# Shift and scale vectors of a two-layer trunk's second layer: partition sums as rows, turned into columns by way of DRAM

## The chip, the cores and the metric

The kernel runs on one core of one Trainium2 chip. The metric is the time of one execution on the device in microseconds, lower is better.

## The reference

A trunk of two layers works on x of 256 rows and 2048 columns, in f32. The token mixer of layer 0 is an attention with forget gates over 16 heads of 128, that of layer 1 a sliding-window attention over 32 query heads of 64. Behind each mixer comes a gated FFN of width 5632 with a convolution over three rows. Both sub-layers of a layer are modulated by vectors that come from a conditioning vector c of 2048 values:

```
c_act = silu(c)
for i in range(2):
    mod = c_act @ ada_w[i] + ada_b[i]                 # ada_w[i]: 2048 x 12288
    sh1, sc1, g1, sh2, sc2, g2 = split(mod, 6)
    y = mixer_i(x * (1 + sc1) + sh1)
    x = layer_norm(alpha * x + (1 + g1) * y)
    y = conv_ffn(x * (1 + sc2) + sh2)
    x = layer_norm(alpha * x + (1 + g2) * y)
```

The change concerns `c_act @ ada_w[1]` for the four vectors sh1, sc1, sh2 and sc2 of layer 1.

## The kernel before, in words

**Weights.** All weights are streamed once from DRAM in f32. `stream` (L277) does it by tiles of two blocks of 128 rows and 512 columns (256 rows of the weight): SP loads `w` (L288) into one of the slots that `wtile` hands out, ACT rounds it to `wh` (L290, f32r), DVE forms the residual `wl = w - wh` (L302), and PE multiplies with both (L76), the first factor being split in the same way. Residuals are recorded two tiles ahead. In the down-projection of the FFN (PE rows `xs<-wh,gT` and `xs<-wl,gT`) the output x is worked off in four d blocks of 512 columns. A tile there is eight matmuls by `wh` and four by `wl`; in the up-projection (`wd`) it is the same number of products in other shapes.

**Between the tiles.** Behind each tile `tick` takes a step of the adaLN work at a set rate, and once per tile `run_post` takes a step of every generator that was handed to `defer`. Such generators carry the additions into x (`residual`, L673): multiply the sum in PSUM by the gate (`t`, L686), add it into x (L687), take statistics (L689).

**The end of a sub-layer.** For the last d block `x_mm_end` (L339) takes the last tiles in another order: row block t = 0 (rows 0 to 127, 512 columns wide) over all of them first, then row block t = 1 in two halves of 256 columns. The last additions into x are pinned on DVE in the order: t = 1 of the tiles before, t = 0 with its statistics and moments (L694), first half, second half with the moments of t = 1. POOL takes the root (`rs`, L698), ACT and DVE normalise x (L714, L716), PE transposes it (L564) between a few dummy matmuls (`warm`), and the modulated h (`hHL`) starts the next sub-layer.

**The adaLN vectors.** `ada_vector` (L442) makes one vector of 2048 values at a time, in the order of `ada_list` (L439): (0,2), (0,3), (0,4), (0,5), (1,0), (1,1), (1,3), (1,2), (1,4), (1,5), layer first. For each block of 128 rows of `ada_w` DVE multiplies by the 128 values of silu(c) and adds into `acc` (128 partitions x 2048, L454 and L456), one half of the row per step. Then the 128 partitions must be summed. Gates (v = 2 and 5) are wanted along the row on every partition: four f32 matmuls with a 128 x 128 block of ones give 128 x 512 each (L469). Shifts and scales (v = 0, 1, 3, 4) are wanted as columns, 128 partitions x 16: for each of 16 pieces of 128 columns one f32 matmul with `acc` as the stationary factor and one column of ones as the moving one, all into one PSUM bank, four of them to a step (L477), and at the end one DVE instruction that adds the bias (`cv`, L481). Both are pinned, that is, they keep their place among the pinned instructions of their engine. `merged` (L743) later makes the modulation's G and B from these columns.

**What sets the order.** The kernel is written in the Tile framework. Its scheduler orders the instructions of each engine; pinned ones keep the order in which they were recorded, others may be moved, and the slots of a pool go to those who ask in scheduled order. PSUM has 8 banks of one pool. In the profile, layer 0's FFN lies between 460 and 1211 us; the sums of (1,0), (1,1) and (1,3) fall into it (first blocks at 798.36, 939.48 and 1092.87), those of (1,4) into layer 1's output projection (first block at 1445.56).

Of the kernel before, what the change touches and what calls it, by code (L numbers as in the profile page):

```python
# [10 lines left out]
F32 = mybir.dt.float32  # L11
# [3 lines left out]
ALU = mybir.AluOpType  # L15
AX = mybir.AxisListType

P = 128
D = 2048
S = 256  # L20
NT = S // P
KC = D // P
# [19 lines left out]
def hybrid_trunk(ctx: ExitStack, tc: tile.TileContext, a: dict, out: bass.AP):  # L42
    nc = tc.nc
# [5 lines left out]
    cst = ctx.enter_context(tc.tile_pool(name="cst", bufs=1))  # L49
# [2 lines left out]
    gp = ctx.enter_context(tc.tile_pool(name="gp", bufs=31))  # L52
    tp = ctx.enter_context(tc.tile_pool(name="tp", bufs=4))
    sp = ctx.enter_context(tc.tile_pool(name="sp", bufs=4))
    psp = ctx.enter_context(tc.tile_pool(name="psp", bufs=8, space=bass.MemoryType.PSUM))

    def wtile(name="w"):
        return wp.tile([P, 2, WB], F32, tag="w", name=name)
# [7 lines left out]
    def bank(name="sm"):  # L66
        return psp.tile([P, 512], F32, tag="ps", name=name)
# [7 lines left out]
    def mm(o, lhsT, rhs, start=False, stop=False, **kw):  # L75
        return nc.tensor.matmul(o, lhsT, rhs, start=start, stop=stop, **kw)  # L76

    def pin(ins, on=True):

        if on:  # L80
            tc.keep_in_program_order(ins)
# [17 lines left out]
    ident = cst.tile([P, P], F32, name="ident")  # L99
# [3 lines left out]
    ones = cst.tile([P, P], F32, name="ones")  # L103
# [20 lines left out]
    pt = bank()  # L124
    nc.tensor.transpose(pt[:, :KC], csil, ident[:KC, :KC])
    nc.vector.tensor_copy(cact, pt[:, :KC])
    acol = cst.tile([P, DEPTH, NADA], F32, name="acol")
    pt = bank()
# [125 lines left out]
    def defer(gen):  # L254

        post.append(gen)
# [180 lines left out]
    cols = {}  # L437
    gates = {}
    ada_list = [(0, 2), (0, 3), (0, 4), (0, 5), (1, 0), (1, 1), (1, 3), (1, 2), (1, 4), (1, 5)]  # L439
    ada = {"gen": None, "debt": 0.0, "rate": 0.0, "gate_free": True}  # L440

    def ada_vector(l, v):  # L442
        row = v % 3 == 2
        acc = cst.tile([P, D], F32, tag="acc", name="acc")
        part = lambda c, n: acc[:, c:c + n]
        step_ = D // 2
        for k in range(KC):
            for c in range(0, D, D // 2):
                w = wtile("wa").rearrange("p a f -> p (a f)")
                pin(nc.sync.dma_start(w, a["ada_w"][l, k * P:(k + 1) * P, v * D + c:v * D + c + D // 2]), False)  # L450
                for o in range(0, D // 2, step_):
                    ac, wo = part(c + o, step_), w[:, o:o + step_]
                    if k == 0:
                        pin(nc.vector.tensor_scalar_mul(ac, wo, cact[:, 0:1]), True)  # L454
                    else:
                        pin(nc.vector.scalar_tensor_tensor(ac, wo, cact[:, k:k + 1], ac,  # L456
                                                           op0=ALU.mult, op1=ALU.add), True)
                yield
        for _ in range(2 if l == 0 else 0):
            yield  # L460
        if row:
            while not ada["gate_free"]:
                yield
            ada["gate_free"] = False
            g = cst.tile([P, D], F32, tag="gate", name="gate")
            nc.gpsimd.dma_start(g, a["ada_b"][l, v * D:(v + 1) * D].partition_broadcast(P))
            for j in range(D // 512):
                ps = bank()
                mm(ps, ones, acc[:, j * 512:(j + 1) * 512], start=True, stop=True)  # L469
                yield  # L470
                gj = g[:, j * 512:(j + 1) * 512]
                nc.vector.scalar_tensor_tensor(gj, ps, 1.0, gj, op0=ALU.add, op1=ALU.add)
            gates[l, v] = g
            return
        ps = bank()
        for k in range(KC):
            pin(mm(ps[:, k:k + 1], part(k * P, P), ones[:, 0:1], start=True, stop=True))  # L477
            if k % 4 == 3:
                yield
        cv = cst.tile([P, KC], F32, tag=f"cv{v}", name="cv")  # L480
        pin(nc.vector.scalar_tensor_tensor(cv, ps[:, :KC], 1.0 if v % 3 else 0.0,  # L481
                                           acol[:, l, v * KC:(v + 1) * KC], op0=ALU.add, op1=ALU.add), True)
        cols[l, v] = cv
        if v == 4:
            ada["held"] = True

    def ada_step():
        if ada["gen"] is None:
            if not ada_list or ada.get("held"):
                return  # L490
            ada["gen"] = ada_vector(*ada_list.pop(0))
        if next(ada["gen"], ada) is ada:
            ada["gen"] = None
# [730 lines left out]
    for t in range(NT):  # L1224
        mu, rs, _ = moments[t]
# [34 lines left out]
```

## Time and profile before

| | us |
|---|---|
| median of 3 runs | 2235.91 |
| lowest and highest | 2234.55, 2236.51 |
| the profiled execution | 2237.59 |
| its span in the profile | 2235.8 |

| engine | busy us | share |
|---|---|---|
| PE (matmul) | 2196.5 | 98% |
| DVE | 1860.3 | 83% |
| ACT | 1193.4 | 53% |
| POOL | 20.3 | 1% |

The granted clock of PE was 0.998 on the mean. A row of the groups gives line, engine, operation and operands (out<-in), the count, then busy time in us, the mean of one in ns, and the idle time ahead of it with what ended it. A row of the timeline gives start, length, and what; neighbours of one kind are merged with their count. An f32 matmul appears as two passes.

### The profile page before, as it was taken

What the parts mean: (1) busy time and instruction counts of PE and PEld (TensorE: products, weight loads), DVE (VectorE), ACT (ScalarE), POOL (GpSimd) and SP (SyncE); (2) the same over time, 40 slices, a digit from 0 to 9 for tenths busy, and PEclk for the clock granted to TensorE, in tenths of its full rate; (3) what the DMA queues carried; (4) which work ended last, traced back from release to release, by engine and by line L of the source; (5) the groups of instructions that cost most, each with busy time, mean ns of one, the idle gap of its engine ahead of it and who ended that gap; (6) DMA issues with size and microseconds to landing.
All of it is one profiled execution on the core that took longest, in us unless ns stands there. A gap on an engine that the chain in (4) does not pass through costs nothing.

```text
span 2235.8 us, 33537 instructions
## 1 busy us (share of the span) xinstructions
PE 2196.5 (98%) x12275; PEld 1890.3 (85%) x12275; DVE 1860.3 (83%) x2705; ACT 1193.4 (53%) x1877; POOL 20.3 (1%) x51
## 2 busy tenths in 40 slices
PE   7999999999999999999999999999999999999998
PEld 6999898788888888888887788888888888888886
DVE  7989998999979968989899888879888655676766
ACT  4546554455556433656534588646655533555642
POOL 0001000000000000000000000000000000000000
PEclk9999999999999999999999999999999999999999
DMA  9999999979878989889798766668887556666553
GB/s 358 391 355 345 356 374 343 308 256 321 310 226 284 339 287 339 280 273 324 257 341 301 233 199 245 216 195 289 284 263 251 182 194 191 192 190 190 189 197 114
DMA packets 287430, 602.69 MB, mean 270 GB/s; under 512 B 21846, under 2 KB 55576, under 8 KB 286752
## 3 DMA queue, kind: packets, MB, share of 16 engines
q1 hardware_dynamic: 286208, 595.86, 78.3%
q0 software_dynamic: 1056, 4.69, 0.6%
q8 instruction: 96, 1.57, 0.3%
q14 instruction: 70, 0.57, 0.1%
HBM read 598.37 MB, written 2.10 MB: 269 GB/s over the span
## 4 chain that ended last, share of the span: by engine, by line
PE 82%; DVE 11%; issue 3%; ACT 2%; DMA 2%; POOL 0%; SPq 0%; DVEq 0%; ACTq 0%; POOLq 0%
PE wd L76 41%; PE xs L76 32%; PE ws L76 4%; DVE acc L456 3%; DVE wl L302 3%; DMA wo<-in_ada_w_dram 2%; PE sm L76 1%; ACT wh L290 1%; PE o L76 1%; PE S L76 1%; ACT pr L775 1%; DVE pr L763 0%; DMA w<-in_fox_w_in_dram 0%; ACT pr L767 0%; PE cps L76 0%
## 5 line engine op out<-in xcount | busy, mean ns | idle before, releaser
L290 ACT CAST wh<-w 128x1024 fp32r<-128x1024 f32 x728 | 764.2, 1052 | 754.5 <-PE wd L76 269.9
L302 DVE TENSOR_TENSOR wl<-w,wh 128x1024 fp32r<-128x1024 f32 x728 | 886.8, 1222 | 281.4 <-ACT wh L290 262.1
L76 PE MATMUL wd<-hHL,wh 128*128 128x512 f32 (+1 forms) x2832 | 718.3, 395 | 0.3
L76 PEld LDWEIGHTS wd<-hHL,wh 128*128 128x128 f32 x2832 | 504.5, 188 | 98.8 <-issue 2.6
L76 PEld LDWEIGHTS wd<-hHL,wl 128*128 128x128 f32 x2816 | 373.1, 188 | 31.4 <-DVE wl L302 0.6
L456 DVE SCALAR_TENSOR_TENSOR acc<-wa,cact,acc 128x1024 f32<-128x1024 f32 x300 | 381.3, 1279 | 0.1
L76 PE MATMUL wd<-hHL,wl 128*128 128x256 f32 x2816 | 379.7, 277 | 0.2 <-DVE wl L302 0.2
L76 PE MATMUL xs<-wh,gT 128*128 128x512 f32 (+1 forms) x1444 | 352.0, 384 | 0.0
L76 PEld LDWEIGHTS xs<-wh,gT 128*128 128x128 f32 x1444 | 266.8, 188 | 53.0
L76 PE MATMUL xs<-wl,gT 128*128 128x512 f32 (+1 forms) x722 | 191.4, 384 | 0.0
L76 PE MATMUL xs<-wh,hHL 128*128 128x512 f32 (+1 forms) x720 | 185.2, 395 | 0.9 <-ACT hHL L85 0.5
L76 PEld LDWEIGHTS xs<-wl,gT 128*128 128x128 f32 x722 | 134.4, 188 | 26.8
L76 PEld LDWEIGHTS xs<-wh,hHL 128*128 128x128 f32 x720 | 128.6, 188 | 28.1 <-issue 1.4
L1147 ACT ACTIVATE u<-s,ccol 128x256 f32<-128x256 f32 x176 | 105.3, 600 | 65.7 <-DVE s L1142 50.0
L76 PE MATMUL ws<-hHL,wh 128*128 128x256 f32 x1024 | 132.0, 281 | 4.9 <-ACT wh L290 2.4
L76 PEld LDWEIGHTS ws<-hHL,wh 128*128 128x128 f32 x1024 | 124.3, 189 | 8.8 <-ACT wh L290 4.2
L76 PE MATMUL xs<-wh,oT 128*128 128x512 f32 (+1 forms) x392 | 101.3, 396 | 0.0
L76 PE MATMUL xs<-wl,hHL 128*128 128x512 f32 (+1 forms) x360 | 97.3, 390 | 1.7 <-DVE wl L302 1.7
L1148 DVE SCALAR_TENSOR_TENSOR u<-s,ccol,u 128x255 f32<-128x255 f32 x176 | 84.1, 479 | 6.2 <-ACT u L1147 6.0
L609 DVE SCALAR_TENSOR_TENSOR oacc<-wo,cact,oacc 128x512 f32<-128x512 f32 x111 | 79.4, 746 | 10.2 <-DMA wo<-in_ada_w_dram 5.4
L1150 DVE SCALAR_TENSOR_TENSOR u<-s,ccol,u 128x254 f32<-128x254 f32 x176 | 84.0, 478 | 1.4
L76 PEld LDWEIGHTS xs<-wh,oT 128*128 128x128 f32 x392 | 71.1, 190 | 13.7 <-DVE oT L86 0.3
(223 smaller groups left out, 1645.2 us busy)
## 6 DMA issues: line engine op xcount, KB each, us to landing
w<-in_ffn_w_up_dram SPq DMA_DIRECT2D x352, 512.0 KB, 4.6
wa<-in_ada_w_dram SPq DMA_DIRECT2D x320, 512.0 KB, 5.1
w<-in_ffn_w_down_dram SPq DMA_DIRECT2D x176, 512.0 KB, 4.6
w<-in_fox_w_in_dram SPq DMA_DIRECT2D x96, 512.0 KB, 6.6
wo<-in_ada_w_dram SPq DMA_DIRECT2D x128, 256.0 KB, 6.7
w<-in_swa_w_in_dram SPq DMA_DIRECT2D x40, 512.0 KB, 5.0
w<-in_fox_w_o_dram SPq DMA_DIRECT2D x32, 512.0 KB, 5.5
w<-in_swa_w_o_dram SPq DMA_DIRECT2D x32, 512.0 KB, 5.3
```

The source lines that it names most:

```text
L76: return nc.tensor.matmul(o, lhsT, rhs, start=start, stop=stop, **kw)
L290: pin(nc.scalar.copy(h, w), casts[0] > 0)
L302: pin(nc.vector.tensor_tensor(l, w, f32(h), op=ALU.subtract), go in behind or tied[0] > 0)
L456: pin(nc.vector.scalar_tensor_tensor(ac, wo, cact[:, k:k + 1], ac, op0=ALU.mult, op1=ALU.add), True)
L609: nc.vector.scalar_tensor_tensor(ac, wk, cact[:, kc:kc + 1], ac, op0=ALU.mult, op1=ALU.add)
L775: nc.scalar.mul(pr[:, b:e], pr[:, b:e], ss[:, r:r + 1])
L1147: nc.scalar.activation(u, s, AF.Identity, bias=cw(CW, f), scale=cw(2, f))
L1148: nc.vector.scalar_tensor_tensor(u[:, 1:], s[:, :S - 1], cw(1, f), u[:, 1:], op0=ALU.mult, op1=ALU.add)
L1150: nc.vector.scalar_tensor_tensor(u[:, 2:], s[:, :S - 2], cw(0, f), u[:, 2:], op0=ALU.mult, op1=ALU.add)
```

## The change

For layer 1 the four shift and scale vectors are summed in another form. For each of four pieces of 512 columns of `acc` one f32 matmul with a single column of ones as stationary factor gives a row of 1 x 512 in a PSUM bank of its own. ACT copies each row to one partition of a tile (`line`, two rows to a tile), and POOL stores two tiles of 1024 values to a scratch row in DRAM. A deferred generator, `turned`, waits a step, has POOL load the 2048 values back as 16 rows of 128 (`lines`), waits three steps more, lets PE transpose them to 128 x 16, and DVE adds the bias. It replaces 64 column matmuls by 16 row matmuls, 16 ACT copies, 8 stores, 4 loads and 4 transposes. Neither the new matmuls nor the new `cv` are pinned. Layer 0's vectors and the gates stay as they are. Line numbers behind the new code are 29 higher in the kernel after, those ahead of it 1 higher.

```
+    dp = ctx.enter_context(tc.tile_pool(name="dp", bufs=2, space=bass.MemoryType.DRAM))
...
+        if l > 0:
+            line, r = dp.tile([D // 1024, 1024], F32, name="line"), None
+            for j in range(D // 512):
+                ps = bank()
+                mm(ps[:1, :], ones[:, :1], part(j * 512, 512), start=True, stop=True)
+                yield
+                r = r if j % 2 else wtile("line")
+                nc.scalar.copy(r[:1, j % 2, :], ps[:1, :])
+                if j % 2:
+                    nc.gpsimd.dma_start(line[j // 2:j // 2 + 1, :], r[:1].rearrange("p a f -> p (a f)"))
+
+            def turned():
+                yield
+                r = wtile("lines")[:KC, 0, :P]
+                nc.gpsimd.dma_start(r, line.rearrange("j (k p) -> (j k) p", p=P))
+                for _ in range(3):
+                    yield
+                pt = bank()
+                nc.tensor.transpose(pt[:, :KC], r, ident[:KC, :KC])
+                cv = cst.tile([P, KC], F32, tag=f"cv{v}", name="cv")
+                nc.vector.scalar_tensor_tensor(cv, pt[:, :KC], 1.0 if v % 3 else 0.0,
+                                               acol[:, l, v * KC:(v + 1) * KC], op0=ALU.add, op1=ALU.add)
+                cols[l, v] = cv
+
+            defer(turned())
+            if v == 4:
+                ada["held"] = True
+            return
         ps = bank()
         for k in range(KC):
             pin(mm(ps[:, k:k + 1], part(k * P, P), ones[:, 0:1], start=True, stop=True))
```

The scheduler also places other instructions differently. Three places matter below.

First, PE behind the last sum of vector (1,0) (`xs` is the down-projection's sum, 8 + 4 matmuls to a weight tile). Before:

```order
L76 MATMUL sm<-ones,acc 128x1 x4
L76 MATMUL xs<-wh,gT 128x512 x8
L76 MATMUL xs<-wl,gT 128x512 x4
L76 MATMUL xs<-wh,gT 128x512 x8
L76 MATMUL xs<-wl,gT 128x512 x4
L76 MATMUL xs<-wh,gT 128x512 x8
```

After:

```order
L77 MATMUL sm<-acc,ones 1x512
L77 MATMUL xs<-wh,gT 128x512 x8
L77 MATMUL xs<-wl,gT 128x512 x4
L77 MATMUL xs<-wh,gT 128x512 x8
L77 MATMUL xs<-wl,gT 128x512 x4
L77 MATMUL xs<-wh,gT 128x512 x8
L77 MATMUL xs<-wl,gT 128x512 x4
L77 MATMUL xs<-wh,gT 128x512 x8
L77 MATMUL xs<-wl,gT 128x512 x4
L77 MATMUL xs<-wh,gT 128x512 x8
L77 MATMUL xs<-wl,gT 128x512 x4
L494 MATMUL sm<-ident,lines 128x16
```

The row sum stands where the last column block stood, and the transpose L494 follows five tiles later; at (1,3) and (1,4) it is five tiles too, at (1,1) six.

Second, DVE in the last part of layer 0's down-projection, where the third d block's sums are added into x while PE works on the fourth (`wl` are residuals for PE's coming tiles, `acc` the adaLN work, `t` a sum times the gate). Before:

```order
L302 TENSOR_TENSOR wl<-w,wh 128x1024
L456 SCALAR_TENSOR_TENSOR acc<-wa,cact,acc 128x1024
L302 TENSOR_TENSOR wl<-w,wh 128x1024 x2
L456 SCALAR_TENSOR_TENSOR acc<-wa,cact,acc 128x1024
L686 TENSOR_TENSOR t<-xs,gate 128x512
L302 TENSOR_TENSOR wl<-w,wh 128x1024
```

After:

```order
L303 TENSOR_TENSOR wl<-w,wh 128x1024
L457 SCALAR_TENSOR_TENSOR acc<-wa,cact,acc 128x1024
L715 TENSOR_TENSOR t<-xs,gate 128x512
L303 TENSOR_TENSOR wl<-w,wh 128x1024
L457 SCALAR_TENSOR_TENSOR acc<-wa,cact,acc 128x1024
L716 TENSOR_TENSOR x<-x,t 128x512
L715 TENSOR_TENSOR t<-xs,gate 128x512
L303 TENSOR_TENSOR wl<-w,wh 128x1024 x2
```

In both, the first `t` shown is the first use of the d block's sums, and the residual just ahead of the last `acc` before it feeds PE's tiles: before, the residuals of two tiles of the next d block stand ahead of that `t`; after, the residual ahead of it is that of the last tile whose sums `t` needs.

Third, PE at the end of layer 0's FFN: tiles of row block t = 0 are 512 wide, halves of t = 1 256 wide. Before, the three tiles of t = 0 and the first of the six half tiles:

```order
L76 MATMUL xs<-wh,gT 128x512 x4
L76 MATMUL xs<-wl,gT 128x512 x2
L76 MATMUL xs<-wh,gT 128x512 x4
L76 MATMUL xs<-wl,gT 128x512 x2
L76 MATMUL xs<-wh,gT 128x512 x4
L76 MATMUL xs<-wl,gT 128x512 x2
L76 MATMUL xs<-wh,gT 128x256 x4
L76 MATMUL xs<-wl,gT 128x256 x2
```

After, from the second tile of t = 0 to just behind the third, with the first tile of t = 0 and one half tile ahead of these rows:

```order
L77 MATMUL xs<-wh,gT 128x512 x4
L77 MATMUL xs<-wh,gT 128x256 x3
L77 MATMUL xs<-wl,gT 128x512 x2
L77 MATMUL xs<-wh,gT 128x256
L77 MATMUL xs<-wl,gT 128x256 x2
L77 MATMUL xs<-wh,gT 128x256 x4
L77 MATMUL xs<-wl,gT 128x256 x2
L77 MATMUL xs<-wh,gT 128x256 x3
L77 MATMUL xs<-wh,gT 128x512 x4
L77 MATMUL xs<-wh,gT 128x256 x3
L77 MATMUL xs<-wl,gT 128x512 x2
L77 MATMUL xs<-wh,gT 128x256
```

The sum of t = 0 ends with the `128x512 x2` near the end of these rows. Behind it stand 12 matmuls of 256 columns after, where there were 36 before. DVE's order there has not changed.

## The prediction

> **What bounds the kernel now.** I read the page first, then the waits of PE, then the timeline at the sums that the change replaces and at the end of layer 0's FFN.
>
> ```profile
> span 2235.8 us, 33537 instructions
> PE 2196.5 (98%) x12275; PEld 1890.3 (85%) x12275; DVE 1860.3 (83%) x2705; ACT 1193.4 (53%) x1877; POOL 20.3 (1%) x51
> PE 82%; DVE 11%; issue 3%; ACT 2%; DMA 2%; POOL 0%; SPq 0%; DVEq 0%; ACTq 0%; POOLq 0%
> ...
> PE xs L76 <- DVE wl L302: 2.7, 4, 1.1
> ...
> DVE cv L481 <- PE sm L76: 12.4, 5, 3.1
> ```
>
> PE is busy 98% of the span and holds 82% of the chain that ended last. In a row of the waits the columns are total, times, longest: over the whole run PE waited 2.7 us for residuals. DVE's 12.4 us ahead of `cv` is time in which DVE sat idle for PE: freeing it gives PE nothing. So the time moves only through work put on PE or taken off it, and through places where PE waits for something new. The sum is made against the profiled execution, 2237.59 us with a span of 2235.8; that is 1.7 above the median of the runs, 2235.91, and the difference I find is added to the median. A measurement here tells a change from none at about 0.2%, 4.5 us.
>
> **PE's own work.** The removed work is 64 column matmuls, 4 to a block. One block, and one of the gate sums, which already have the row form (512 moving f32 columns, K of 128):
>
> ```profile
> 795.63 1.98 PE L76 MATMUL xs<-wh,gT 128*128 128x512 f32 x8
> 797.44 1.08 PE L76 MATMUL xs<-wl,gT 128*128 128x512 f32 x4
> 798.36 0.95 PE L76 MATMUL sm<-ones,acc 128*128 128x1 f32 x8
> 799.17 2.09 PE L76 MATMUL xs<-wh,gT 128*128 128x512 f32 x8
> ...
> 635.17 2.02 PE L76 MATMUL wd<-hHL,wh 128*128 128x512 f32 x8
> ...
> 637.94 1.02 PE L76 MATMUL sm<-acc,ones 128*128 128x512 f32 x2
> 638.40 2.43 PE L76 MATMUL wd<-hHL,wh 128*128 128x512 f32 x8
> ...
> 1202.76 1.07 PE L76 MATMUL xs<-wh,gT 128*128 128x512 f32 x4
> 1203.67 0.61 PE L76 MATMUL xs<-wl,gT 128*128 128x512 f32 x2
> ...
> L76 PE MATMUL xs<-wh,gT 128*128 128x512 f32 x1372 | 340.5, 390 | 0.0
> L76 PE MATMUL sm<-acc,ones 128*128 128x512 f32 x32 | 16.2, 591 | 0.0
> L166 PE MATMUL sm<-ident,rows 88*128 88x88 f32 x8 | 0.9, 239 | 0.0
> ```
>
> Columns of the timeline: start, length, what; each f32 matmul shows as two passes. A block's price is the time from its start to where the eight matmuls behind it would have begun had they taken their usual length. For the columns that is 799.17 + 2.09 − 1.98 − 798.36 = 0.92; for a row sum 638.40 + 2.43 − 2.02 − 637.94 = 0.87. Both times 16: 14.7 and 13.9, so 0.8 off PE, and with 0.05 read either way on each block, from 1.6 off to none. The group row agrees in kind: 16.2/32 = 0.51 busy to a pass, where an f32r matmul of the same 512 columns has 340.5/1372 = 0.25 (and a pitch of (1203.67 − 1202.76)/4 = 0.227). Four transposes come in, nearest the one of `rows`, 239 ns alone; I take 0.15 each in the queue, +0.6 in all. **PE's work: −0.2.**
>
> The Trainium skill, "TensorE: Matmul & The Clock Gate", section "Wait — 56ns, not 53.3ns?", gives N ÷ 2.4 GHz + 2.5 ns between back-to-back matmuls, 216 ns at N of 512; by it a block of two passes would be an estimated 0.43 us. The trace disagrees, with 0.87 for the gate's block. Rival 3 prices such a rate from rows.
>
> **The detour through DRAM.** Per vector: four copies on ACT, two stores, one load, a transpose. In the orders shown with the change the transpose stands five tiles behind the last row sum, at (1,1) six. A tile is 12 matmuls at 0.227 = 2.72 us, so the row has 13.6 us (16.3 at (1,1)) to come back, and PE waits for what is over. What it needs:
>
> ```profile
> L290 ACT CAST wh<-w 128x1024 fp32r<-128x1024 f32 x728 | 764.2, 1052 | 754.5 <-PE wd L76 269.9
> ...
> L992 ACT COPY part<-ws 128x512 f32<-128x512 f32 x8 | 4.3, 590 | 4.2 <-PE ws L76 4.2
> ...
> gate<-in_ada_b_dram POOLq DMA_DIRECT2D x4, 1024.0 KB, 8.2
> ...
> out_dram<-x SPq DMA_DIRECT2D x7, 256.0 KB, 2.1
> ...
> rows<-in_ffn_conv_b_dram POOLq DMA_DIRECT2D x2, 44.0 KB, 4.2
> ...
> rows<-in_ln_ffn_g_dram POOLq DMA_DIRECT2D x1, 16.0 KB, 5.5
> ...
> sink<-in_swa_sinks_dram POOLq DMA_DIRECT2D x1, 16.0 KB, 8.6
> ```
>
> The copy is 0.59, and I allow 0.9 for the better part of a cast (1.05) ahead of it on ACT. No transfer to a scratch row in DRAM is in the trace; the small ones from POOL land 4.2 to 5.5 us after issue, and the 8.6 stands behind a load of `gate`. Stores of the result from SP land in 2.1. I take 5.3 for a store and 5.3 for a load, near the 5.5 of the row nearest in size: 0.6 + 0.9 + 5.3 + 5.3 = 12.1 us, so 1.5 us are left and PE does not wait. At 2.1 + 4.2 the row is back in 7.8; at 8.6 each in 18.7, which costs up to 5.1 at three of the vectors and 2.4 at (1,1). POOL has 1% to do, and nothing stands behind the waiting load there but the next vector's stores. The 16 copies are 9.4 us on ACT, 53% busy, and hide behind PE. **Zero here**, 0 to +18 as bounds.
>
> The Trainium skill, "DMA: Bandwidth & Descriptors", section "Anatomy of one DMA — SWDGE (gpsimd) path", gives about 2.0 us plus bytes / 436e3 for a transfer from POOL, so an estimated 4 us for store and load; it adds that completion "can cause a surprisingly long delay especially when the write target is HBM". The trace's rows of 4.2 and more are above its 2.0.
>
> **What the scheduler moves elsewhere.** 16 more PSUM allocations and 12 more tiles let the order differ in places that the diff does not touch. Two of them count. The rows for both, a window of DVE's share, then DVE and PE from the timeline:
>
> ```profile
> 1160.00:1190.00 30.00, 30.00 (x134) 24.86 (x133) 27.67 (x28) 11.62 (x11) 0.00 (x0) 1.00 0.90 332
> ...
> 1181.00 0.68 DVE L686 TENSOR_TENSOR t<-xs,gate 128x512 f32<-128x512 f32 x1
> 1181.60 1.22 DVE L302 TENSOR_TENSOR wl<-w,wh 128x1024 fp32r<-128x1024 f32 x1
> 1182.73 0.68 DVE L687 TENSOR_TENSOR x<-x,t 128x512 f32<-128x512 f32 x1
> 1183.34 0.68 DVE L686 TENSOR_TENSOR t<-xs,gate 128x512 f32<-128x512 f32 x1
> ...
> 1184.54 1.27 DVE L456 SCALAR_TENSOR_TENSOR acc<-wa,cact,acc 128x1024 f32<-128x1024 f32 x1
> 1185.72 1.22 DVE L302 TENSOR_TENSOR wl<-w,wh 128x1024 fp32r<-128x1024 f32 x1
> ...
> 1204.12 0.64 PE L76 MATMUL xs<-wh,gT 128*128 128x256 f32 x4
> ...
> 1208.43 1.78 PE L76 MATMUL warm<-ones 128*128 128x512 f32 x7
> ...
> 1211.47 0.76 PE L564 MATMUL sm<-ident,x 128*128 128x128 f32 x4 [0.35 <-DVE x L716]
> ...
> 1204.51 0.68 DVE L686 TENSOR_TENSOR t<-xs,gate 128x512 f32<-128x512 f32 x1
> ...
> 1206.86 0.36 DVE L686 TENSOR_TENSOR t<-xs,gate 128x256 f32<-128x256 f32 x1
> ...
> 1207.71 0.43 DVE L689 BATCH_NORM_STATS2 stats<-x 128x6 f32<-128x256 f32 x1
> 1208.63 0.42 DVE L686 TENSOR_TENSOR t<-xs,gate 128x256 f32<-128x256 f32 x1 [0.49 <-PE xs L76]
> ...
> 1210.01 0.29 DVE L694 BATCH_NORM_AGGREGATE mv<-stats 128x2 f32<-128x30 f32 x1
> ```
>
> First, DVE in layer 0's down-projection, where the third d block's sums are added into x. The `t` that waits for PE's last sum now has no residual ready behind it for the next tiles; before, two more stood ahead of it, one behind the other.
>
> (Columns of the window: length, busy of PE, PEld, DVE, ACT, POOL, then clock, DMA share, GB/s: DVE 27.67 of 30.) With starts to starts of 0.60 (`t`, `x`), 1.13 (`wl`) and 1.18 (`acc`), and G the end of the old block on PE, `t` begins at G − 0.25: two matmuls of t = 1 (0.45) follow on PE behind the sum it reads, and DVE starts 0.20 after a sum (1208.43 to 1208.63). So the second residual ends at G − 0.25 + 0.60 + 1.13 + 1.18 + 0.60 + 0.60 + 1.22 = G + 5.1. PE wants it after one tile and the 8 of the next: 2.72 + 1.81 = G + 4.5. **+0.6**, from 0 to 1; other blocks, with one residual more, stay whole by as little as 0.6, for which the range gets another 1.
>
> Second, the end of that FFN: the second and third of the 512-wide tiles of t = 0 now stand among the halves of t = 1. All of it stays, but t = 0 ends later, with 12 matmuls of 256 (0.12 each) behind it instead of 36.
>
> The halves take 1204.12 to 1208.43, 4.31 for 36. With 12 behind it, t = 0 ends at 1208.43 − 1.44 = 1207.0, 2.9 later. DVE's order here is pinned and unchanged: t = 0 takes 1204.51 to 1206.86 (2.35), the first half to some 1208.1 (1.28), the second 1208.63 to 1210.30 (1.67). Before, DVE was idle 0.49 ahead of the last; now from 1207.2 on there is no gap: 1207.2 + 2.35 + 1.28 + 1.67 = 1212.5, against 1210.3. The normalised x, for which PE already waits at 1211.47, is 2.2 later. **+2.2**, from 1.5 to 3: PE's dummy matmuls, `warm`, cover none of it.
>
> Sum: −0.2 + 0 + 0.6 + 2.2 = **+2.6 us**; 2235.91 + 2.6 = 2238.5, and 2240.2 for an execution like the profiled one.
>
> **Rivals.**
> 1. *The row is back too late* (slower). At 8.6 us a transfer, three waits of about 5 and one of 2.4 come on top of 2.6: 18 + 2.6, 2256; at 7 each (chain 15.5) 1.9 three times, 2244. It decides where store and load pass 12.1 us together. For it: the 8.6 row, and a store to be received before the load may start. Against it: that row's gate load, and 1% on POOL. 0.20 in all, mostly the small end.
> 2. *DVE's lead is lost in more blocks* (slower): the FFN has four d blocks per layer; it decides where two residuals and what stands between them on DVE pass the 4.5 us above, and a misplaced `t` and `acc` cost 0.60 + 1.18, so two more such places give 2242. Against it: PE waited 2.7 us in all for residuals. 0.12.
> 3. *Row sums at the f32r pitch* (faster): two passes of 0.227 are 0.45 a block where 0.87 was taken, 6.7 us off the forecast, so 2231.8. Against it the gate's block and its 0.51 a pass. 0.05.
> 4. *The moved order costs nothing* (no change): if DVE's chain at the FFN's end has slack that I don't see, or PE's order is decided by waits, only PE's work counts: 2235.7. For it: that nearly cancels. Against: PE did wait at 1211.47. 0.18.
>
> The forecast itself has 0.45. Faster by over 0.2% needs rival 3 or a detour that frees more than I see: 0.06. Within: the forecast's most part and rival 4, 0.58. Slower: rivals 1 and 2 and the forecast's upper end, 0.36. The range leaves out rival 3 and the far end of rival 1: 2234.5 (rival 4 with PE's work at −1.6 + 0.6, and half a microsecond of the median's own spread) to 2247.
>
> **What would show it.** In the profile after: `sm<-acc,ones` of 1 × 512 at about 506 ns a pass; no wait of L494 for the lines' load; the load landing within 12.1 us of the last row sum; `t` of t = 0 near the FFN's end 2.9 later against its halves, and L593 waiting for x by 2.2 more than the 0.35 before; one wait of `xs` for `wl` of some 0.6 near 1185. Wrong if the L494 rows wait, if row passes show 250 ns, or if the end of the FFN takes from the last `xs` to the first `hHL` product what it took.

## The result, and the profile after

| | us |
|---|---|
| after: median of 6 runs | 2247.38 (2247.11 to 2248.96) |
| before: median of the 6 runs beside them | 2237.02 |
| ratio of the two, 95% interval | 1.0048 (1.0037 to 1.0059) |
| after: profiled execution, span | 2248.33, 2246.6 |

One of the six runs of before lies far off at 2724.5 us; the ratio leaves it out. The change costs 0.48%, 10.7 us, where I had forecast 2.6 and a range that ends at 2247.0.

The page and the waits of PE and DVE after; a row of the waits has total, times, longest:

```profile
span 2246.6 us, 33418 instructions
PE 2204.1 (98%) x12183; PEld 1878.5 (84%) x12183; DVE 1857.7 (83%) x2705; ACT 1200.8 (53%) x1893; POOL 26.3 (1%) x63
...
PE sm L593 <- ACT x L743: 3.3, 1, 3.3
PE xs L77 <- DVE wl L303: 3.1, 5, 1.1
...
DVE t L715 <- PE xs L77: 40.2, 19, 5.7
```

PE's busy time has grown by 7.6 us, a new wait of 3.3 us stands ahead of the transposes of x, and DVE waits 40.2 us for sums at `t` (18.4 before).

To place the loss I compared the starts of ACT's casts, 919 in each kernel and most of them one to a weight tile, between the two profiles. What the lag behind the kernel before grows by in each stretch is in the first column of numbers here; the other columns are the experiments below.

| stretch (us in the profile of before) | after | e1 | e2 | e3 | e4 | e5 | e6 | e7 | e8 |
|---|---|---|---|---|---|---|---|---|---|
| sums of (1,0), 794.9 to 842.2 | 1.36 | 0.24 | 1.36 | 1.36 | 1.35 | 4.71 | 1.57 | 0 | 0 |
| sums of (1,1), to 1068.1 | 1.44 | 0.22 | 1.41 | 1.44 | 1.43 | 1.44 | 1.65 | 0 | 0 |
| sums of (1,3), to 1147.7 | 1.38 | 0.25 | 1.38 | 1.37 | 1.38 | 1.37 | 1.59 | 0 | −0.1 |
| third d block, to 1191.2 | 0.80 | 0.80 | 0.75 | 0 | 0 | 0.77 | 0.80 | 0 | 0 |
| end of layer 0's FFN, to 1247.2 | 4.41 | 5.24 | 5.33 | 2.00 | 0.16 | 4.61 | 4.42 | 2.22 | 0.18 |
| sums of (1,4), 1436.7 to 1542.6 | 1.39 | 0.24 | 1.40 | 1.42 | 1.38 | 1.39 | 1.61 | 0 | 0 |

The column of after adds up to 10.8. All else is equal within 0.3 us, but for the first 795 us of a profiled execution, which differ by −3.3 to +0.6 from before. Of the difference, 1.6 to 2.2 us arise between 440 and 463 us in e1 to e6 and e8: there PE's granted clock fell in the profiles of before, after and e7 (0.60, 0.57 and 0.61 on the mean from 443 to 447 us) and in no other. Whole times carry that difference, the stretches do not.

**The sums.** PE's timeline at (1,0), columns start, length, what. Before, the column block behind the one that the prediction shows at 798.36:

```profile
802.02 0.95 PE L76 MATMUL sm<-ones,acc 128*128 128x1 f32 x8
```

After:

```profile
797.55 1.07 PE L77 MATMUL xs<-wl,gT 128*128 128x512 f32 x4
798.55 1.02 PE L77 MATMUL sm<-acc,ones 128*1 128x512 f32 x2
799.50 2.12 PE L77 MATMUL xs<-wh,gT 128*128 128x512 f32 x8
801.46 1.07 PE L77 MATMUL xs<-wl,gT 128*128 128x512 f32 x4
802.45 1.02 PE L77 MATMUL sm<-acc,ones 128*1 128x512 f32 x2
...
826.75 1.07 PE L77 MATMUL xs<-wl,gT 128*128 128x512 f32 x4
827.75 0.23 PE L494 MATMUL sm<-ident,lines 16*128 16x16 f32 x1
827.91 2.14 PE L77 MATMUL xs<-wh,gT 128*128 128x512 f32 x8
829.89 1.08 PE L77 MATMUL xs<-wl,gT 128*128 128x512 f32 x4
```

A block and a tile took 802.02 − 798.36 = 3.66 us before, and take 802.45 − 798.55 = 3.90 now. Less the tile's 2.72 a column block cost 0.94 and a row block costs 1.18, where I had taken 0.87. The gap is on both sides of the block, not within it: the row sum starts 1.00 after the start of the four matmuls ahead of it (0.91 without a block), the eight behind it start 0.95 after it, where I had taken 0.87, and 1.96 lie from their start to the next group (801.46 − 799.50), where eight alone take 1.81. The transpose holds the same pattern: 1.00 ahead of it (827.75 − 826.75), and 829.89 − 827.75 = 2.14 from its start over the eight matmuls behind it, which alone take 1.81. No row here has a wait; the page counts all of it as PE busy.

**The detour.** Issues from POOL on the page after, the last number being the median to landing:

```profile
line<-line POOLq DMA_DIRECT2D x8, 4.0 KB, 1.9
lines<-line POOLq DMA_DIRECT2D x4, 8.0 KB, 4.4
```

A store lands in 1.9 us, a load in 4.4, and no transpose waits for one.

**The third d block and the end of the FFN.** PE and DVE in the timeline after:

```profile
1188.02 1.99 PE L77 MATMUL xs<-wh,gT 128*128 128x512 f32 x8
1190.45 1.21 PE L77 MATMUL xs<-wl,gT 128*128 128x512 f32 x4 [0.44 <-DVE wl L303]
...
1211.66 0.63 PE L77 MATMUL xs<-wl,gT 128*128 128x512 f32 x2
...
1218.65 1.12 PE L593 MATMUL sm<-ident,x 128*128 128x128 f32 x4 [3.32 <-ACT x L743]
```

```profile
1178.82 1.28 DVE L457 SCALAR_TENSOR_TENSOR acc<-wa,cact,acc 128x1024 f32<-128x1024 f32 x1
1185.03 0.69 DVE L715 TENSOR_TENSOR t<-xs,gate 128x512 f32<-128x512 f32 x1 [4.93 <-PE xs L77]
...
1213.02 0.68 DVE L715 TENSOR_TENSOR t<-xs,gate 128x512 f32<-128x512 f32 x1
1213.74 0.69 DVE L716 TENSOR_TENSOR x<-x,t 128x512 f32<-128x512 f32 x1
1214.35 0.68 DVE L715 TENSOR_TENSOR t<-xs,gate 128x512 f32<-128x512 f32 x1
```

And DVE's share from there to the FFN's end (length, then busy PE, PEld, DVE):

```profile
1185.00:1213.00 28.00, 27.56 (x136) 23.01 (x136) 27.97 (x27) 9.08 (x9) 0.00 (x0) 1.00 0.82 284
```

In the bracket stands the idle time ahead of an instruction and what ended it. DVE stood idle for 4.93 us at `t`, with residuals and adaLN work queued behind it; before, `t` started at 1181.00 with no idle time at all. Then DVE is full to the FFN's end, 27.97 of 28 us. At earlier d blocks of the changed kernel DVE stands idle for `t` as long, 4.76 us at 802.1, 3.53 at 838.7 and 5.10 at 871.4, and the stretches show no loss from it; what differs at the third block is that DVE has no idle time left ahead of the FFN's end. PE has the sum of t = 0 ready at 1211.66 + 0.45 = 1212.1, but DVE takes it at 1214.35.

### The profile page after: what moved, and what is told of

Same layout as the page of the kernel before. It is cut to its first block, busy times and chain, and to the rows that moved or that the text cites. A ratio compares the mean times of both kernels' runs of the same rounds, so it can differ in the third digit from the quotient of the medians.

```text
span 2246.6 us, 33418 instructions
## 1 busy us (share of the span) xinstructions
PE 2204.1 (98%) x12183; PEld 1878.5 (84%) x12183; DVE 1857.7 (83%) x2705; ACT 1200.8 (53%) x1893; POOL 26.3 (1%) x63
```

## The experiments

Two theories and their rivals. **S**: a stationary factor (the operand that is loaded into PE ahead of a matmul) smaller than 128 x 128 (the single column of ones, the 16 rows of the transposed tile) makes PE lose time on both sides; rival: the blocks wait for something else. **T2**: DVE's 4.93 idle us come out at the end of the FFN, since DVE has nothing free between; rival **T1**, the prediction's: PE's mixed order there sets the end.

**e1: row sums with the full block of ones.**

```
-                mm(ps[:1, :], ones[:, :1], part(j * 512, 512), start=True, stop=True)
+                mm(ps, ones, part(j * 512, 512), start=True, stop=True)
```

> The row sums with a full 128 x 128 block of ones as stationary factor, so that the sum lands on all 128 partitions as for the gates; ACT still copies one row. Theory S (a stationary factor of one column makes PE load and drain outside of its usual overlap, 1.18 us a block instead of the gate's 0.87): 16 x 0.31 = 5.0 us faster than the changed kernel, about 2242.4, and the blocks' period with one tile falls from 3.90 to 3.59 us. Rival (the block's price is set by waits on the PSUM bank or on ACT's copy, whatever the shape): no change, about 2247.4.

2244.66 us, 1.0037 times the kernel before (1.0023 to 1.0050). This interval overlaps that of the changed kernel (1.0037 to 1.0059), so the reading rests on the stretches. PE's order is that of the changed kernel throughout, DVE's at the places shown. PE's timeline of e1:

```profile
796.32 1.02 PE L77 MATMUL sm<-acc,ones 128*128 128x512 f32 x2
796.77 2.41 PE L77 MATMUL xs<-wh,gT 128*128 128x512 f32 x8
799.02 1.08 PE L77 MATMUL xs<-wl,gT 128*128 128x512 f32 x4
799.94 1.02 PE L77 MATMUL sm<-acc,ones 128*128 128x512 f32 x2
```

The period is 3.62, as S expected, and each vector's lag falls from about 1.4 to 0.24. Of the expected 5.0 us the four vectors give 4.6; the whole time fell by 2.7 (five runs from 2242.5 to 2245.1), and the FFN's end cost 0.8 more than in the profile of the changed kernel. The rival falls by the period.

The loads of the stationary factors (PEld) fit that. PEld in the timeline after, then in e1:

```profile
798.55 0.09 PEld L77 LDWEIGHTS sm<-acc,ones 128*1 128x1 f32 x2 [0.35 <-issue]
799.50 1.69 PEld L77 LDWEIGHTS xs<-wh,gT 128*128 128x128 f32 x8 [0.86 <-issue]
```

```profile
796.09 0.42 PEld L77 LDWEIGHTS sm<-acc,ones 128*128 128x128 f32 x2
```

With one column the load starts with its matmul (798.55 both), as does the next full load (799.50 both). With the full block it starts 0.23 ahead of its matmul, under the work before.

**e2: PE's order at the FFN's end pinned** (every matmul that `x_mm_end` records for its last tiles).

```
+        if tail[0]:
+            tc.keep_in_program_order(i)
...
+            tail[0] = True
             x_mm(ps, kc, h, l, stat, nk - 1, ts=(0,))
...
+            tail[0] = False
```

> The changed kernel with PE's order at the end of each long sum pinned as it is recorded, so that row block t = 0 ends ahead of the halves as before the change; DVE's order stays that of the changed kernel. Theory T1 (the prediction's: PE's late end of t = 0 sets the end of the FFN): 2.2 to 4.4 us faster, 2243.0 to 2245.2. Theory T2 (DVE arrives there 4.7 us late, since it stood idle 4.93 us ahead of the third d block's product with the gate and has no idle time left to make it up): no change, about 2247.4, and DVE's addition for t = 0 starts at 1214.4 as before.

2249.62 us, 1.0057 (1.0045 to 1.0070): not faster. PE and DVE in the timeline of e2:

```profile
1206.19 0.63 PE L77 MATMUL xs<-wl,gT 128*128 128x512 f32 x2
...
1216.13 1.12 PE L600 MATMUL sm<-ident,x 128*128 128x128 f32 x4 [3.40 <-ACT x L750]
```

```profile
1211.82 0.68 DVE L722 TENSOR_TENSOR t<-xs,gate 128x512 f32<-128x512 f32 x1
```

The sum of t = 0 is there at 1206.19 + 0.45 = 1206.6, five microseconds before DVE takes it. DVE, not PE's order, sets the end. T1 falls as the cause in the changed kernel.

**e3: the third d block's products with the gate pinned on DVE**, which puts them behind the residuals again.

```
-            pin(nc.vector.tensor_tensor(tmp, p[:, :n], gate[:, c0 + a0:c0 + a1], op=ALU.mult), end)
+            pin(nc.vector.tensor_tensor(tmp, p[:, :n], gate[:, c0 + a0:c0 + a1], op=ALU.mult), end or (last and d == 2))
```

> The changed kernel with the third d block's products with the gate pinned among DVE's instructions, so that three to four residuals stand ahead of them as before the change; PE's order at the FFN's end is still mixed. T2: the 0.8 us stall of PE goes and DVE is on time, so that PE's late t = 0 sets the end with 2.2 us instead of 4.4: 3.0 us faster, about 2244.4. T1: only the stall goes, about 2246.6.

2242.44 us, 1.0029 (1.0018 to 1.0041), 4.9 below the changed kernel. Part of that is the first 795 us, which ran 2.9 us shorter in its profile than in that of the changed kernel; in the stretches the third d block costs nothing and the FFN's end 2.00 instead of 4.41, 3.2 in sum, as T2 expected. DVE in the timeline of e3:

```profile
1208.64 0.69 DVE L715 TENSOR_TENSOR t<-xs,gate 128x512 f32<-128x512 f32 x1 [1.73 <-PE xs L77]
```

Now it is DVE that waits for PE's t = 0: with DVE on time the mixed order costs 2.00 us, close to the prediction's 2.2.

**e4: both orders restored** (the edits of e2 and e3).

> Both of the two orders restored. T2 and T1 alike: the whole loss at the FFN's end and the stall go, 0.8 + 4.4 = 5.2 us faster, about 2242.2, still slower than the kernel before by the price of the sums, 5.4 us. If it is slower than that, a third cause is at work at the end of the FFN.

2240.30 us, 1.0020 (1.0011 to 1.0029). The FFN's end costs 0.16, the third block nothing, and the four vectors still 5.5. No third cause there.

**e5: the transpose without its waiting steps.**

```
-                for _ in range(3):
-                    yield
                 pt = bank()
```

> The changed kernel without the three waiting steps ahead of the transpose, which then stands two to three tiles behind the last row sum instead of five to six. Theory D (the row's way through DRAM is hidden only by that distance): by the landings in the profile of the changed kernel PE waits about 5.7 us at vector (1,0) and 0 to 1 at the other three, 6.6 us slower than the changed kernel in all, about 2254. Rival (the row is back long before it is asked for): no wait of PE at the transposes, about 2247.4.

2249.87 us in its one run. The waits of PE in e5:

```profile
PE sm L494 <- DMA lines<-line: 3.3, 1, 3.3
```

One wait, at (1,0), of 3.3 us: the mechanism of D, with half of its size. The row was back 11.1 us after the start of the last row sum, 12.3 in the changed kernel's profile, and the transpose came 1.2 us later than I had placed it, since part of the next tile's matmuls stand ahead of it. So the three steps do hide the detour, at (1,0) with 2.5 us to spare in the changed kernel's profile: its load lands 5.4 after its issue at 819.85, the transpose starts at 827.75.

**e6: 64 columns of ones** (`ps[:64, :]` and `ones[:, :64]` in the row sum).

> The row sums with 64 columns of ones as stationary factor instead of 1 (changed kernel) or 128 (the first experiment). Theory S in its narrow form (any stationary factor smaller than 128 x 128 falls out of the overlap): a block and a tile have a period of 3.90 us as with one column. Rival (only very narrow ones do, or the price falls with the width): a period between 3.62 and 3.90; 3.62 is that of the full block.

2246.99 us in its one run. PE's timeline of e6:

```profile
796.52 1.07 PE L77 MATMUL sm<-acc,ones 128*64 128x512 f32 x2
...
800.47 1.07 PE L77 MATMUL sm<-acc,ones 128*64 128x512 f32 x2
```

3.95 us, no better than with one column. Yet S is worded too widely: not every factor smaller than 128 x 128 pays. PE's timeline before holds a transpose of 96 rows amid full matmuls, and one of 2 rows:

```profile
183.54 1.07 PE L76 MATMUL ws<-hHL,wl 128*128 128x256 f32 x8
184.45 0.25 PE L151 MATMUL sm<-ident,rows 96*128 96x96 f32 x1
184.48 2.13 PE L76 MATMUL ws<-hHL,wh 128*128 128x256 f32 x16
186.45 1.11 PE L76 MATMUL ws<-hHL,wl 128*128 128x256 f32 x8
...
374.43 1.07 PE L76 MATMUL xs<-wl,oT 128*128 128x512 f32 x4
375.43 0.22 PE L181 MATMUL sm<-ident,posf 2*128 2x2 f32 x1
```

The one of 96 rows starts with no gap (184.45 − 183.54 = 0.91 for eight; the 16 ahead of these took 1.81), and 2.00 lie from its start over the 16 matmuls behind it: it costs 0.19, where one of 16 rows cost 0.42. The one of 2 rows starts 1.00 after four matmuls that alone take 0.91, as the row sums do. So factors of 1 and 64 columns and of 2 and 16 rows pay here, and one of 96 rows does not; where between 64 and 96 that begins, no run shows.

**e7: the kernel before, with four spare products on DVE at the third d block.**

```
+        if last and d == 2:
+            thirds[0] += 1
+            if thirds[0] == 2:
+                spare = ttile()
+                for _ in range(4):
+                    pin(nc.vector.tensor_tensor(spare, gate[:, c0:c0 + 512], gate[:, c0:c0 + 512], op=ALU.mult))
```

> The kernel before, not the changed one, with four spare products of 128 x 512 on DVE (0.60 us each, their result unused) pinned around the third d block's additions in layer 0's down-projection. Theory T2 (DVE has no idle time from there to the FFN's end beyond 0.49 us, so what it loses there comes out at the end of the FFN): 2.4 - 0.5 = 1.9 us slower, 2237.7, all of it between PE's last sum of the FFN and the next sub-layer. Rival (DVE makes it up, or PE's order at the end was the cause): no change, 2235.8.

2238.72 us, 1.0010 (1.0000 to 1.0019) against 2236.70 for the kernel before. PE's timeline of e7:

```profile
1212.20 0.66 PE L564 MATMUL sm<-ident,x 128*128 128x128 f32 x4 [1.40 <-ACT x L721]
```

The lag is 0.6 up to the FFN's last tile and 2.8 behind it. 2.4 us of work far ahead of the end, with PE's order as it was and not one new stall of PE on the way, come out as 2.2 us there. T2 holds without the change.

**e8: everything taken back but the form** (e1, e2 and e3, and the transpose over 128 partitions of a zeroed tile).

```
-                r = wtile("lines")[:KC, 0, :P]
-                nc.gpsimd.dma_start(r, line.rearrange("j (k p) -> (j k) p", p=P))
+                r = wide
+                nc.gpsimd.dma_start(r[:KC], line.rearrange("j (k p) -> (j k) p", p=P))
...
-                nc.tensor.transpose(pt[:, :KC], r, ident[:KC, :KC])
+                nc.tensor.transpose(pt[:, :P], r, ident)
```

> The changed kernel with all known causes taken back: full 128 x 128 ones for the row sums, the transposes over all 128 partitions of a zeroed tile of which 16 rows are loaded, and both orders restored. S and T2 together: row blocks at 0.90 (columns had 0.94) and transposes at about 0.15 instead of 0.41, so that sums and detour cost what the columns did; with 0.2 left at the FFN's end about 2236, no slower than the kernel before by more than 0.5 us. If it stays 2 us or more above it, a cause is still missing.

2235.22 us against 2236.70, 0.9993 (0.9984 to 1.0001): no difference from the kernel before that these runs can tell. PE's timeline of e8 at the transpose:

```profile
825.90 0.27 PE L504 MATMUL sm<-ident,wide 128*128 128x128 f32 x1
825.92 2.09 PE L77 MATMUL xs<-wh,gT 128*128 128x512 f32 x8
827.86 1.08 PE L77 MATMUL xs<-wl,gT 128*128 128x512 f32 x4
```

1.96 to the next group, 0.15 more than the eight alone, where 16 rows took 2.14, and was held up 0.09 ahead of it: 0.42 against 0.15. With sums and transposes in full shape the four vectors cost what the columns did. So the 10.8 us of the stretches are accounted for as far as these runs tell, and the detour through DRAM, which e8 keeps, has no part in them.

## Why the prediction was wrong, point by point

**PE's work, −0.2 (from −1.6 to none, and 0.6 for the transposes): wrong, +5.5.** This is the step that failed first, and half of the loss. I priced the row sum by the gate's, "which already have the row form (512 moving f32 columns, K of 128)", and looked only at the moving side; the stationary one has one column here and 128 there. Sixteen blocks at 1.18 instead of the columns' 0.94 are 3.8, four transposes at 0.42 are 1.7. The bounds could not hold it, because both rows they came from had full stationary factors. For the transposes I took 0.15 from the row of `rows`, whose shape is 88*128; the price was in reach not there but at `posf`, with the shape 2*128 and the gap of 0.09 ahead of it that e6 above shows. The Trainium skill, "TensorEngine Tiling (Array Packing)", section "Key Properties", says that changing the tiling mode drains TensorE. e1 and e6 fit it, with 0.28 us a block between 128*1 and 128*128 and nothing gained with 128*64, and so does the transpose of 96 rows that starts without a gap; that PE drains there, and when it changes its mode, no run shows. I had not weighed that rule.

**The detour, zero: right.** I had 12.1 us for copy, store and load; at (1,0) the last copy starts at 814.03 and the load lands at 825.2, 11.2 later. The last store took 4.3 there and the load 5.4, close to the 5.3 that I took for each; at the other vectors the last store took 1.6 to 2.1. The 8.6 of rival 1 did not come.

**DVE at the third d block, +0.6: right, 0.80.** PE waited 0.44, as worked out, and the matmuls just around the wait took 0.36 more than in a full stream.

**The end of the FFN, +2.2: wrong, 4.41.** The term itself is measured in e3, 2.00. What failed is the sentence "DVE's order here is pinned and unchanged": the order is, but I let DVE come to it at the time that it had before. The same move of `t` that I had just priced at 0.6 for PE also left DVE idle for 4.93 us, and my own row, 27.67 of 30 us busy, said that DVE could not make that up. I priced the late residual and not the lost time of a full engine. Since DVE came later than PE's late sum, the order of PE that I took for the cause cost nothing more in the changed kernel (e2). The two do not add: PE's order alone gives 2.0 (e3), DVE's lateness alone 5.3 (e2), both together 4.4: the later one counts, and that e2's 5.3 is more than 4.4 goes with a longer stretch at a low clock, told of below.

**Rivals.** Rival 2 named the right place, DVE's lead, with the wrong price: it counted further stalls of PE along the way, of which there were none, though DVE stood idle for `t` at three more d blocks, and not the end. Rival 3 fell, 0.43 us a pass is what the trace shows in every form. Rival 4 fell with e3 and e4. The range ended 0.4 us below the median, and it reached that far only through rival 1, which did not come: that it was missed by so little is luck. It had no term for a small stationary factor and none for DVE's lateness.

## What to carry to other kernels

Price a matmul by a row with the same tile shape on both sides, and by the starts of its neighbours, not by its own busy time: a lone matmul whose stationary factor had 1 or 64 columns, or 2 or 16 rows, among full ones was paid for here ahead of it and behind it as well, and shows as busy. Where an engine is full up to the point at which the next sub-layer waits for it, idle time that a new order gives it upstream is owed there, and where it has idle time left, it is not; ask of each moved instruction not only who waits for it, but how long its own engine will stand. Two late inputs to one chain do not add, so undoing one of them may show nothing.

## What the runs showed of the hardware that I had not expected

A matmul with a stationary factor of 128 x 1 or 128 x 64 amid 128 x 128 ones costs 0.28 to 0.33 us more than a full one with the same moving columns; a transpose of 16 rows costs 0.27 more than one of 128 (0.42 against 0.15), and one of 96 rows about as little as one of 128 (0.19).

PE's clock fell after the longer wait. Two windows of the profile after, with the granted clock as the third number from the end:

```profile
1215.00:1220.00 5.00, 1.68 (x8) 1.25 (x6) 4.28 (x11) 2.71 (x6) 1.51 (x3) 0.83 0.86 286
1220.00:1225.00 5.00, 4.91 (x22) 3.59 (x21) 4.23 (x11) 3.59 (x7) 0.21 (x1) 0.82 1.04 417
```

One window of e1, then one of e2:

```profile
1215.00:1220.00 5.00, 4.91 (x18) 4.00 (x19) 4.47 (x12) 3.19 (x6) 0.00 (x0) 0.67 1.03 424
```

```profile
1215.00:1220.00 5.00, 3.79 (x13) 2.84 (x14) 3.69 (x10) 4.24 (x8) 1.16 (x2) 0.50 1.04 386
```

The window ahead has 0.99 in e1 and 0.97 in e2, the one behind 1.00 and 0.85; e2's 0.50 is the low clock itself. A window of 5 us with a mean clock c then spent 10 (1 − c) us at it: 1.7 + 1.8 = 3.5 us after, 0.1 + 3.3 = 3.4 in e1, 0.3 + 5.0 + 1.5 = 6.8 in e2. So e2 has twice as much of it, and e1 as much as the changed kernel, but later. After the idle time of 3.32 us at L593 four transposes take 1.12 us in the changed kernel, in e1 0.66 behind the same 3.32, and only the next four 1.12; behind 1.32 to 1.40 us of idle time in e3 and e7 the four take 0.66, and the clock stays at 1.00. Between the two fours PE waits 0.93 us in e1 and hardly at all in the changed kernel, so there the slow transposes cover a wait, and in e1 they do not. That fits the 0.8 to 0.9 by which the FFN's end costs more in e1 and e2; that the clock is the whole of it was not tried. The Trainium skill, "TensorE: Matmul & The Clock Gate", section "Why this matters for your kernels", asks for no idle gaps of PE over about 3 us; the waits of 3.32 and 3.40 agree. The fall at 443 us in before and after, told of with the stretches, does not follow from it: there PE was never idle for more than 0.7 us at a time in the 18 us ahead. What brought it about is open.
